# The first matrix product of six SwiGLU blocks computed as seven half-size products instead of eight

## The chip, the cores and the metric

The kernel runs on one core of a Trainium2 chip. The metric is the time of one execution on the device in microseconds (us); lower is better. Inputs and outputs lie in HBM. All arithmetic is in float32 or in pairs of float32r numbers.

## The reference, cut to what matters

The program is two stacks of layers over 512 tokens of width 1024. The first stack has two layers, each with a feed-forward block (FFN), a mixer and a second FFN, with a layer norm behind each; the second stack has two layers, each with a mixer and one FFN. So there are six FFNs, all of one shape, and they are what the change touches:

```python
D_MODEL = 1024; SEQ = 512; D_FF = 2816          # D_FF_2 of the second stack is 2816 too

def swiglu(x, w_in, w_out):
    gu = x @ w_in                               # 512x1024 by 1024x5632
    g, u = gu[..., :D_FF], gu[..., D_FF:]
    return (jax.nn.silu(g) * u) @ w_out         # 512x2816 by 2816x1024

# first stack, l = 0, 1
x = layer_norm(ALPHA * x + 0.5 * swiglu(x, ffn_w_in[l, 0], ffn_w_out[l, 0]), ln_g[l, 0], ln_b[l, 0])
x = layer_norm(ALPHA * x + mixer(x), ln_g[l, 1], ln_b[l, 1])
x = layer_norm(ALPHA * x + 0.5 * swiglu(x, ffn_w_in[l, 1], ffn_w_out[l, 1]), ln_g[l, 2], ln_b[l, 2])
# second stack, l = 0, 1
h = h + mixer_2(rms_norm(h, norm_mix[l]))
h = h + swiglu(rms_norm(h, norm_ffn[l]), w_ffn_in[l], w_ffn_out[l])
```

## The kernel before, in words

**Layout.** Activations lie transposed: eight tiles of 128 features by 512 tokens. `x` is the float32 value, `xh` and `xl` its two float32r parts (`split`: ScalarE copies to float32r, which gives the high part, VectorE subtracts it, which gives the low part). The tokens come in two halves, `HA` (0 to 255) and `HB` (256 to 511). A weight is split in the same way into `wh` and `wl`, and one product of two such numbers is three matmuls (`mm3`, lines 204 to 208): `wh` by `xh`, `wh` by `xl`, `wl` by `xh`. The weight is the stationary operand, the tokens move, and each matmul loads 128 by 128 weights of its own.

**An FFN** (`ffn`, line 272). The 2816 features of gate and of up are 22 tiles of 128 rows each. A weight unit is one tile of gate or up over all 1024 inputs: 128x1024 numbers, 512 KB, loaded by one DMA on SP's queue into one of three buffers `wr`, and split into one of three pairs `wh`, `wl`. A unit is 8 times `mm3`, 24 matmuls of 512 columns. When the up unit of a tile is done, `gate` makes silu(gate) on ScalarE (`sg`, line 281), the product with up on VectorE (`hf`, line 283) and its split `hh`, `hl`. `pre` (line 216) does the first four units in two passes, all of `HA` and then all of `HB`, in matmuls of 256 columns, because the norm of the layer ahead (`tail`, in the classes `LN` and `RMS`) ends with `HA` first and with `HB` while TensorE works on `HA`; the other 40 units are done by `gemms`, with the whole 512 tokens. Then `out_gemm` multiplies `hh`, `hl` by `w_out`.

**What sets the order.** The functions emit the work in one order with a clock of their own (`tick`, `run`); a scheduler of the framework then orders the instructions of each engine and sets the waits. VectorE, ScalarE and SP's queue work strictly in that order.

The FFNs are called from `program`: the first at the kernel's start, the second behind the first mixer, the third straight behind the second, the fourth behind the second mixer, the fifth and sixth in the second stack, with RMS norms, where `x` is the residual and the normed input lies in `xh` and `xl` alone.

Of the kernel before, what the change touches and what calls it, by code (L numbers as in the profile page):

```python
# [17 lines left out]
T = 512  # L18
D = 1024
KD = 8  # L20
NM = 22
# [3 lines left out]
HA, HB, HT = slice(0, 256), slice(256, 512), slice(0, 512)  # L25
# [6 lines left out]
FT = 2  # L32
PACE2, Y3 = 2.0, 1.0
MP, MF = 4, 3
AP, AF_, AK = 2, 3, 1
NP = 4
PACE = 2.0

SLOTS = [h for p in [(i, i + 4) for i in range(4)] + [(i + 8, i + 12) for i in range(4)] for h in p]
# [17 lines left out]
class Core:  # L57
# [128 lines left out]
    def weights(self, src, n=1024, at=None):  # L186

        w = self.raw(src, n)
        if at:
            for i in range(0, n, T):  # L190
                m = min(T, n - i)
                self.split(at[0][i // T][:, :m], at[1][i // T][:, :m], w[:, i:i + m])
            h, l = at
        else:
            h = self.wsp.tile([128, 1024], F32R, name="wh")
            l = self.wsp.tile([128, 1024], F32R, name="wl")
            self.split(h[:, :n], l[:, :n], w[:, :n])
        self.a(n)
        self.v(n)
        return h, l  # L200

    def mm3(self, out, w, k, xh, xl, start, stop):
        mm = self.nc.tensor.matmul
        wh, wl = (a[k // 4][:, k % 4 * 128:k % 4 * 128 + 128] if isinstance(a, tuple) else a[:, k * 128:(k + 1) * 128]
                  for a in w)
# [10 lines left out]
    def pre(self, srcs, ats=()):  # L216
# [12 lines left out]
        return ps  # L229
# [39 lines left out]
                            yield 0.65 * n / 512  # L269
                j[3](ps)  # L270

    def ffn(self, w_in, w_out, half, post, tail=None):

        nc, tc = self.nc, self.tc
        with tc.tile_pool(name="h", bufs=1) as hp:
            hh = [hp.tile([128, T], F32R, name=f"hh{m}") for m in range(NM)]
            hl = [hp.tile([128, T], F32R, name=f"hl{m}") for m in range(NM)]

            def gate(m, pg, pu):
                sg = hp.tile([128, T], F32, name="sg", bufs=2)  # L280
                nc.scalar.activation(sg, pg, AF.Silu)
                hf = hp.tile([128, T], F32, name="hf", bufs=2)
                nc.vector.scalar_tensor_tensor(hf, pu, half, sg, op0=OP.mult, op1=OP.mult)  # L283
                self.split(hh[m], hl[m], hf)
            first = [(m, j) for m in range(3) for j in range(2)][:NP]
            ats = [tuple(tuple(a[m:m + 2]) for a in (hh, hl)) for m in range(NM - 2, NM - 2 * (NP - 2), -2)]
            p0 = dict(zip(first, self.pre([w_in[m, :, j] for m, j in first], ats)))
            pend = {}

            def cb(m, j):  # L290
                def f(p):
                    pend[j] = p
                    if j:
                        gate(m, pend[0], p)
                return f
            for (m, j), p in p0.items():
                cb(m, j)(p)
# [4 lines left out]
    def out_gemm(self, w_out, hh, hl, nk, post, tail):  # L302

        self.run((self.out_head(w_out, hh, hl, nk, post, KD - tail), 1.0))
        self.out_tail(w_out, hh, hl, nk, post, tail)

    def out_part(self, o, u, w, hh, hl, s, first, last):
# [12 lines left out]
        if d == head - 1:  # L320
            self.later(post.mid(self, head), "mid")

    def out_head(self, w_out, hh, hl, nk, post, head):
        post.begin(self)
        seq = [(d, (i, min(i + 8, nk))) for d in range(head) for i in range(0, nk, 8)]
        held = {}
        for i, u in enumerate(seq):
            for v in seq[i:i + 2]:
                if v not in held:
                    held[v] = self.out_load(w_out, v)  # L330
            if i == len(seq) - 1:
                self.first_tail(w_out, nk, head)
            d, (k0, k1) = u
            if k0 == 0:
# [1185 lines left out]
def program(tc, d, out):  # L1520
    with ExitStack() as ctx:
        c = Core(ctx, tc, d["consts"])
        nc = tc.nc
        w0 = c.raw(d["w_in"][0][0, :, 0], 1024)
        c.ahead.append(w0)
        c.load_x(d["xT"], HA)

        def behind():
            c.load_x(d["xT"], HB)
            c.load_consts()  # L1530
        c.behind = behind
        b2 = Block2(ctx, c)
        with tc.tile_pool(name="b2t", bufs=1) as S:
            c.fill(S, 1216)
            c.later(b2.setup(S), "setup")
            c.ffn(d["w_in"][0], d["w_out"][0], 0.5, LN(c, 0))
            c.flush("setup")
        mlstm(c, d["ml_gate"], d["ml_qk"], d["ml_v"], d["ml_o"], d["ml_out"], LN(c, 1))
        c.ffn(d["w_in"][1], d["w_out"][1], 0.5, LN(c, 2))
        c.ffn(d["w_in"][2], d["w_out"][2], 0.5, LN(c, 3))  # L1540
        attn(c, d["at_q"], d["at_k"], d["at_v"], d["at_out"], LN(c, 4))
        c.ffn(d["w_in"][3], d["w_out"][3], 0.5, LN(c, 5, RMS(c.k("mix_g", 0, 8))), T4)
        for l in range(2):
            w = {n: d["b_" + n][l] for n in ("hf", "hq", "hg", "c", "hi", "nq", "kk", "vv", "w1", "out", "rope")}
            b2.layer(l, w, RMS(c.k("ffn_g", 8 * l, 8)))
            c.ffn(d["b_win"][l], d["b_wout"][l], 1.0, Out(out) if l else RMS(c.k("mix_g", 8, 8)))


def _ct(a, n=128):
# [125 lines left out]
```

## Time and profile before

| | us |
|---|---|
| median of 3 runs | 3350.05 (3348.68 to 3352.29) |
| profiled execution | 3350.13 |
| its span, first to last instruction | 3348.3 |
| TensorE matmul busy | 3305.9 (99% of the span), 18704 matmuls |
| TensorE weight load busy | 2827.0 (84%), beside the matmuls |
| VectorE busy | 1686.3 (50%) |
| ScalarE busy | 1280.9 (38%) |
| mean granted TensorE clock | 0.996 |

How to read it: a time in the timeline is from the start of the span; the duration of a matmul is longer than the distance to the next one's start, because matmuls are pipelined, so what a stream of them costs is read from the starts. `b` is a PSUM bank. A time in brackets is the engine's idle time ahead of an instruction, with what ended it.

### The profile page before, as it was taken

To read this page: it belongs to the slowest core of one execution; us is meant where nothing else is said; L and a number is where in the kernel's file an instruction comes from. 1 tells how busy PE (TensorE), PEld (TensorE's weight loads), DVE (VectorE), ACT (ScalarE), POOL (GpSimd) and SP (SyncE) were. 2 spreads that over 40 slices of the span, in tenths; PEclk is the share of its full clock that TensorE was granted. 3 is DMA by queue.
4 is the path that set the end of the run, shared out by engine and by line. 5 is a ranking of instruction groups with operands and counts; after the bars stand their busy time and mean duration, and the time that the engine had idled before them with its cause. 6 is when DMAs were issued, how large, how long until landed. Compare 5 with 4: busy or idle time off the path is not lost.

```text
span 3348.3 us, 46248 instructions
## 1 busy us (share of the span) xinstructions
PE 3305.9 (99%) x18704; PEld 2827.0 (84%) x18704; DVE 1686.3 (50%) x3451; ACT 1280.9 (38%) x2231; POOL 96.1 (3%) x138
## 2 busy tenths in 40 slices
PE   8999999999999999999999989999999999999999
PEld 7888977988898888879888978788888988898888
DVE  4333756733354333787334667775333567853332
ACT  3322545522233222685222433563232335632221
POOL 0000011000000000110000000000000000000000
PEclk9999999999999999999999989999999999999999
DMA  4333322233332333212333523112333332023333
GB/s 143 96 94 97 100 76 64 89 97 98 93 109 89 100 94 108 74 41 89 95 98 98 163 88 94 45 51 82 99 95 94 107 115 64 26 72 102 98 101 95
DMA packets 88918, 304.04 MB, mean 91 GB/s; under 512 B 9857, under 2 KB 12417, under 8 KB 88705
## 3 DMA queue, kind: packets, MB, share of 16 engines
q1 hardware_dynamic: 88704, 301.10, 29.3%
q8 instruction: 146, 2.39, 0.3%
q14 instruction: 68, 0.55, 0.0%
HBM read 298.96 MB, written 2.10 MB: 90 GB/s over the span
## 4 chain that ended last, share of the span: by engine, by line
PE 94%; DVE 3%; ACT 2%; DMA 1%; issue 1%; POOL 0%; DVEq 0%; SPq 0%; ACTq 0%; POOLq 0%
PE b L206 26%; PE b L208 26%; PE b L207 26%; PE b L267 2%; PE b L268 2%; PE b L266 2%; PE b L1250 1%; PE b L1442 1%; PE b L1391 1%; PE b L1420 1%; PE b L716 1%; ACT wh L174 1%; DVE wl L177 1%; PE b L1303 1%; DMA wr<-w_in 1%
## 5 line engine op out<-in xcount | busy, mean ns | idle before, releaser
L174 ACT ACTIVATE wh<-wr 128x1024 fp32r<-128x1024 f32 (+3 forms) x532 | 545.0, 1026 | 1568.1 <-PE b L207 980.5
L177 DVE TENSOR_TENSOR wl<-wr,wh 128x1024 fp32r<-128x1024 f32 (+3 forms) x532 | 628.3, 1183 | 867.2 <-ACT wh L174 864.9
L206 PE MATMUL b<-xh,wh 128*128 128x512 f32 (+1 forms) x2712 | 1021.7, 378 | 9.5 <-ACT xh L174 7.4
L208 PE MATMUL b<-xh,wl 128*128 128x512 f32 (+1 forms) x2712 | 1008.8, 373 | 3.2 <-DVE wl L177 3.2
L207 PE MATMUL b<-xl,wh 128*128 128x512 f32 (+1 forms) x2712 | 1008.7, 373 | 2.9 <-DVE xl L177 1.8
L206 PEld LDWEIGHTS b<-xh,wh 128*128 128x128 f32 x2712 | 511.1, 189 | 105.5 <-issue 9.4
L208 PEld LDWEIGHTS b<-xh,wl 128*128 128x128 f32 x2712 | 512.5, 189 | 94.5 <-DVE wl L177 5.8
L207 PEld LDWEIGHTS b<-xl,wh 128*128 128x128 f32 x2712 | 513.1, 189 | 91.7 <-issue 3.5
L206 PE MATMUL b<-hh,wh 128*128 128x512 f32 (+1 forms) x1144 | 400.4, 350 | 0.0
L208 PE MATMUL b<-hh,wl 128*128 128x512 f32 (+1 forms) x1144 | 398.4, 348 | 0.0
L207 PE MATMUL b<-hl,wh 128*128 128x512 f32 (+1 forms) x1144 | 398.3, 348 | 0.0
L283 DVE SCALAR_TENSOR_TENSOR hf<-b,sg 128x512 f32<-128x512 f32 x132 | 90.7, 691 | 407.4 <-PE b L208 404.0
L206 PEld LDWEIGHTS b<-hh,wh 128*128 128x128 f32 x1144 | 216.5, 189 | 28.6 <-issue 1.0
L207 PEld LDWEIGHTS b<-hl,wh 128*128 128x128 f32 x1144 | 216.5, 189 | 28.5 <-issue 1.0
L208 PEld LDWEIGHTS b<-hh,wl 128*128 128x128 f32 x1144 | 216.5, 189 | 27.6
L267 PE MATMUL b<-wl,xh 128*128 128x512 f32 (+2 forms) x352 | 122.8, 349 | 4.3 <-DVE wl L177 4.2
L266 PE MATMUL b<-wh,xh 128*128 128x512 f32 (+2 forms) x352 | 125.1, 360 | 0.0
L268 PE MATMUL b<-wh,xl 128*128 128x512 f32 (+2 forms) x352 | 122.7, 349 | 0.0
L177 DVE TENSOR_TENSOR hl<-hf,hh 128x512 fp32r<-128x512 f32 x132 | 89.9, 685 | 0.0
L174 ACT ACTIVATE hh<-hf 128x512 fp32r<-128x512 f32 x132 | 82.8, 632 | 0.8
L1395 ACT ACTIVATE sc<-sc,nm 128x128 f32<-128x128 f32 (+3 forms) x128 | 71.1, 557 | 23.5 <-DVE nm L1393 22.5
L267 PEld LDWEIGHTS b<-wl,xh 128*128 128x128 f32 x352 | 67.2, 191 | 14.3 <-DVE wl L177 6.1
(408 smaller groups left out, 4122.1 us busy)
## 6 DMA issues: line engine op xcount, KB each, us to landing
wr<-w_in SPq DMA_DIRECT2D x176, 512.0 KB, 3.7
wr<-b_win SPq DMA_DIRECT2D x88, 512.0 KB, 3.7
wr<-w_out SPq DMA_DIRECT2D x80, 512.0 KB, 3.5
wr<-b_wout SPq DMA_DIRECT2D x36, 512.0 KB, 3.5
wr<-w_out SPq DMA_DIRECT2D x36, 384.0 KB, 3.1
wr<-b_out SPq DMA_DIRECT2D x20, 512.0 KB, 3.6
wr<-b_w SPq DMA_DIRECT2D x16, 512.0 KB, 3.8
wr<-b_wout SPq DMA_DIRECT2D x16, 384.0 KB, 3.2
```

Of the source, the lines that this page charges most:

```text
L174: nc.scalar.activation(h, src, AF.Copy)
L177: nc.vector.tensor_sub(l, src, h.bitcast(F32))
L206: mm(out, wh, xh, start=start, stop=False)
L207: mm(out, wh, xl, start=False, stop=False)
L208: mm(out, wl, xh, start=False, stop=stop)
L266: mm(ps[t][:, :n], self.xh[k][:, ts], wh, start=k == 0, stop=False)
L267: mm(ps[t][:, :n], self.xh[k][:, ts], wl, start=False, stop=False)
L268: mm(ps[t][:, :n], self.xl[k][:, ts], wh, start=False, stop=k == KD - 1)
L283: nc.vector.scalar_tensor_tensor(hf, pu, half, sg, op0=OP.mult, op1=OP.mult)
L716: nc.tensor.matmul(p[:, :257], w[:, (j - j0) * 128:(j - j0 + 1) * 128], v[s][:, h], start=s == ss[0], stop=s == ss[-1])
L1250: nc.tensor.matmul(p[:, i * 64:(i + 1) * 64], K[h][:, ts], q, start=True, stop=True)
L1395: nc.scalar.activation(sc[:, :N], sc[:, :N], AF.Exp, bias=nm[:, g:g + 1], scale=-1.0, accum_out=sm[:, g:g + 1])
```

## The change

In every FFN 20 of the 22 tiles (ten pairs of tiles, `p` = 1 to 10) are computed by a scheme of seven products. Gate and up weights of a pair, each in two halves of the inputs, are the four blocks of a 2x2 matrix (`g(0)`: gate, inputs 0 to 511; `g(1)`: gate, the others; `g(2)`, `g(3)`: up); the input, in two halves of the inputs and two of the tokens, is the other (`b11` to `b22`). A product (`p1` to `p7`) is 256 rows by 512 inputs by 256 tokens: 2 times 4 times `mm3`, 24 matmuls of 256 columns, into one PSUM bank. Four sums of weights (`s2` and three in place, 128x1024 each) and eleven operations on the results (seven sums, two products and two copies or silus beside them) are made per pair, nearly all on VectorE. The results `h` stay float32 until the end of the loop and are then split by `halves`, ten times 128x1024. Four sums of the input (`t1` to `t4`, in `stage`) are made while `pre` works on `HB`; `t4` takes the place of `xh`, `xl` of the features 0 to 511 of `HB` once `pre` has read them. In the second stack the input is put together from `xh` and `xl` (`whole`) behind the end of each half. Weights come by DMAs of two times 512 numbers per row, through seven buffers. Tile pair 0 is still done by `pre`.

```diff
     def weights(self, src, n=1024, at=None):
         w = self.raw(src, n)
-        if at:
+        if at and not isinstance(at[0], tuple):
+            h, l = at
+            self.split(h[:, :n], l[:, :n], w[:, :n])
+        elif at:
...
         for s in (HA, HB):
             self.flush(s.start)
+            if then:
+                then(s)
             for k in range(KD):
...
-            self.run((self.gemms([("a", w_in[m, :, j], cb(m, j)) for m in range(NM) for j in range(2)
-                                  if (m, j) not in p0]), 1.0))
-            self.out_gemm(w_out, hh, hl, NM, post, tail or FT)
+            def whole(s):
+                for i, n in enumerate(parts):
+                    k0, t = parts[n]
+                    if normed and t is s:
+                        staged[n] = wide(f"h{1 + i}", dt=F32)
+                        for k in range(4):
+                            nc.vector.tensor_add(staged[n][:, k * 256:k * 256 + 256], self.xh[k0 + k][:, t].bitcast(F32),
+                                                 self.xl[k0 + k][:, t].bitcast(F32))
+            def stage():
...
+                for k in ks:
+                    sub(q("t1", k), g("b11", k), g("b12", k))
+                for k in ks:
+                    sub(q("t3", k), g("b22", k), g("b12", k))
+                for k in ks:
+                    stt(q("t2", k), q("t1", k), -1.0, g("b22", k), op0=OP.mult, op1=OP.subtract)
+                put("t2")
+                for k in ks:
+                    stt(q("t4", k), q("t2", k), -1.0, g("b21", k), op0=OP.mult, op1=OP.subtract)
+                put("t3")
+                put("t1")
+                staged["t4"] = o["t4"]
...
+            def weight(st):
+                p, x = st
+                g = lambda q: raws[p, q]
+                if x == "p6":
+                    held["s2", p] = wide("s2", dt=F32)
+                    nc.vector.tensor_add(held["s2", p], g(0), g(3))
+                elif x == "p5":
+                    nc.vector.tensor_add(g(2), g(2), g(3))
...
+                wh = self.wsp.tile([128, 1024], F32R, name="wh")
+                wl = self.wsp.tile([128, 1024], F32R, name="wl")
+                self.split(wh, wl, src)
+                if x == "p2":
+                    nc.vector.tensor_add(g(0), g(0), g(2))
+                elif x == "p7":
+                    nc.vector.tensor_add(g(1), g(1), held.pop(("s2", p)))
...
+            def product(st, w):
+                p, x = st
+                P[x] = self.bank()
+                for m in range(2):
+                    for k in range(4):
+                        wk = tuple(a[:, m * T + k * 128:m * T + k * 128 + 128] for a in w)
+                        self.mm3(P[x][:, m * 256:m * 256 + 256], wk, None, *moving(x, k), k == 0, k == 3)
+                        self.tick(0.36)
...
+            steps = [(p, x) for p in (1, 2) for x in ("p1", "p2")]
+            steps += [(p, x) for p in (1, 2) for x in ("p6", "p7", "p5", "p3", "p4")]
+            steps += [(p, x) for p in range(3, NP2) for x in ("p1", "p2", "p6", "p7", "p5", "p3", "p4")]
...
+            def then(s):
+                whole(s)
+                if s is HB:
+                    fetch()
+                    ahead(0, 2)
+                    stage()
...
+            for i, st in enumerate(steps):
+                ahead(i, 3)
+                product(st, ready.popleft())
+                after(st)
+                if i == len(steps) - 3:
+                    loaded[units[0]] = self.out_load(w_out, units[0])
+                    halves(5)
+                elif i == len(steps) - 2:
+                    loaded[units[1]] = self.out_load(w_out, units[1])
+                    halves(9)
+            self.out_gemm(w_out, hh, hl, NM, post, tail or FT, loaded, halves)
```

VectorE in the middle of the loop of the first FFN, before: one period, a gate tile and an up tile; `wl` is the low part of a weight unit.

```order
L177 TENSOR_TENSOR wl<-wr,wh 128x1024
L283 SCALAR_TENSOR_TENSOR hf<-b,sg 128x512
L177 TENSOR_TENSOR wl<-wr,wh 128x1024
L177 TENSOR_TENSOR hl_185<-hf,hh_163 128x512
L177 TENSOR_TENSOR wl<-wr,wh 128x1024
```

VectorE at the same place after: part of one pair. L377 (not shown) makes `s2`, L388, L379 and L386 are the sums of weights in place, L176 the low parts, the others work on results of products.

```order
L388 TENSOR_TENSOR wr<-wr,s_2169 128x1024
L176 TENSOR_TENSOR wl<-s_2169,wh 128x1024
L176 TENSOR_TENSOR wl<-wr,wh 128x1024
L417 TENSOR_TENSOR ga<-ua,b 128x512
L379 TENSOR_TENSOR wr<-wr,er 128x1024
L420 TENSOR_TENSOR ua<-ua,b 128x512
L176 TENSOR_TENSOR wl<-wr,wh 128x1024 x2
```

Two tiles took VectorE four low parts and four smaller operations; a pair now takes it seven low parts, four sums of weights and nine smaller operations.

VectorE at the start of the second FFN, before: the norm of `HB` ends with `xl_103` (feature tile 7), and the next are the low parts and gates of the loop.

```order
L465 TENSOR_TENSOR x_87<-x_87,b 128x256
L471 TENSOR_TENSOR xl_102<-x_86,xh_94 128x256
L471 TENSOR_TENSOR xl_103<-x_87,xh_95 128x256
L177 TENSOR_TENSOR wl<-wr,wh 128x1024
L283 SCALAR_TENSOR_TENSOR hf<-b,sg 128x512 x2
L177 TENSOR_TENSOR wl<-wr,wh 128x1024
```

The same place after, first where the norm of `HB` begins (L656 and L657 are its first two steps, 464 and 465 of before; `xl_96` is feature tile 0):

```order
L650 TENSOR_TENSOR lnr<-lnst,lnr 128x2
L176 TENSOR_TENSOR wl<-wr,wh 128x1024
L663 TENSOR_TENSOR xl_102<-x_86,xh_94 128x256
L386 TENSOR_TENSOR wr<-wr,er 128x1024
L663 TENSOR_TENSOR xl_103<-x_87,xh_95 128x256
L656 TENSOR_TENSOR x_80<-x_80,b 128x256
L176 TENSOR_TENSOR wl<-wr,wh 128x1024
L657 TENSOR_TENSOR x_80<-x_80,b 128x256
L656 TENSOR_TENSOR x_81<-x_81,b 128x256
L377 TENSOR_TENSOR s_6627<-wr,er 128x1024
L663 TENSOR_TENSOR xl_96<-x_80,xh_88 128x256
```

Four operations of 128x1024 now stand ahead of the first finished tile of `HB`. Then, where the norm has ended (`h_6418` is `t4`):

```order
L332 SCALAR_TENSOR_TENSOR h_6418<-h_6416,x_87 128x256
L176 TENSOR_TENSOR t3l<-h_6417,t3h 128x1024
L176 TENSOR_TENSOR t1l<-h_6415,t1h 128x1024
L176 TENSOR_TENSOR t2l<-h_6416,t2h 128x1024
L176 TENSOR_TENSOR xl_96<-h_6418,xh_88 128x256
L176 TENSOR_TENSOR xl_97<-h_6418,xh_89 128x256
L176 TENSOR_TENSOR xl_98<-h_6418,xh_90 128x256
L176 TENSOR_TENSOR xl_99<-h_6418,xh_91 128x256
L464 SCALAR_TENSOR_TENSOR ga<-b,ga 128x512 x2
L176 TENSOR_TENSOR wl<-wr,wh 128x1024
```

The last row is the low part of the weights of the third product (`p1` of pair 2); the low parts of the first two products stand in the piece above it, and the whole of `stage` and the gates of tiles 0 and 1 stand ahead of the third.

## Rows read from the trace of the kernel before

**Rows 1.** The page: busy time of engines, and the last chain by engine.

```profile
PE 3305.9 (99%) x18704; PEld 2827.0 (84%) x18704; DVE 1686.3 (50%) x3451; ACT 1280.9 (38%) x2231; POOL 96.1 (3%) x138
...
PE 94%; DVE 3%; ACT 2%; DMA 1%; issue 1%; POOL 0%; DVEq 0%; SPq 0%; ACTq 0%; POOLq 0%
```

**Rows 2.** Waits of TensorE: total us, times, longest; the three largest.

```profile
PE b L206 <- ACT xh L174: 7.4, 2, 6.4
PE b L398 <- DVE lns L489: 6.2, 1, 6.2
PE b L267 <- DVE wl L177: 4.2, 2, 2.1
```

**Rows 3.** Timeline, TensorE, loop of the first FFN: start, duration, instruction; 16 matmuls.

```profile
59.50 0.39 PE L208 MATMUL b<-xh,wl 128*128 128x512 f32 x1
...
63.12 0.39 PE L206 MATMUL b<-xh,wh 128*128 128x512 f32 x1
```

**Rows 4.** Timeline, TensorE, `pre` of the second FFN: its last 15 matmuls.

```profile
648.12 0.28 PE L206 MATMUL b<-xh,hh 128*128 128x256 f32 x1
...
649.80 0.28 PE L208 MATMUL b<-xh,hl 128*128 128x256 f32 x1
```

**Rows 5.** Timeline, VectorE, loop of the first FFN: a low part and the next instruction.

```profile
58.12 1.22 DVE L177 TENSOR_TENSOR wl<-wr,wh 128x1024 fp32r<-128x1024 f32 x1 [0.15 <-ACT wh L174]
59.26 0.68 DVE L177 TENSOR_TENSOR hl<-hf,hh 128x512 fp32r<-128x512 f32 x1
```

**Rows 6.** Timeline: VectorE's smaller operations, each row a run back to back; ScalarE's copy.

```profile
349.78 2.47 DVE L438 TENSOR_TENSOR x<-x,b 128x512 f32<-128x512 f32 x4
...
624.32 0.75 DVE L442 TENSOR_TENSOR x<-x,b 128x256 f32<-128x256 f32 x2
...
62.47 1.06 ACT L174 ACTIVATE wh<-wr 128x1024 fp32r<-128x1024 f32 x1 [3.83 <-PE b L207]
```

**Rows 7.** Timeline, VectorE, start of the second FFN: the norm of `HB`, first and last.

```profile
634.15 0.16 DVE L458 TENSOR_TENSOR lnr<-lnst,lnr 128x2 f32<-128x2 f32 x1 [0.81 <-POOL lnr L457]
...
645.45 0.42 DVE L471 TENSOR_TENSOR xl<-x,xh 128x256 fp32r<-128x256 f32 x1 [0.70 <-ACT x L469]
```

**Rows 8.** The same at the start of the third FFN: end of the norm, then the loop.

```profile
1013.66 0.43 DVE L471 TENSOR_TENSOR xl<-x,xh 128x256 fp32r<-128x256 f32 x1 [0.70 <-ACT x L469]
1018.22 1.23 DVE L177 TENSOR_TENSOR wl<-wr,wh 128x1024 fp32r<-128x1024 f32 x1 [4.13 <-ACT wh L174]
```

**Rows 9.** Timeline, VectorE and TensorE, start of the fifth FFN (RMS norm).

```profile
2290.80 0.99 DVE L177 TENSOR_TENSOR xl<-sq,xh 128x256 fp32r<-128x256 f32 x2
...
2301.76 0.28 PE L208 MATMUL b<-xh,hl 128*128 128x256 f32 x1
```

**Rows 10.** Timeline, VectorE, start of the first FFN.

```profile
34.27 1.23 DVE L177 TENSOR_TENSOR wl<-wr,wh 128x1024 fp32r<-128x1024 f32 x1 [12.29 <-ACT wh L174]
```

**Rows 11.** Stretches: length; busy us of PE, PEld, DVE, ACT, POOL; clock, DMA share, GB/s.

```profile
1965.00:1966.00 1.00, 0.00 (x0) 0.00 (x0) 0.97 (x3) 0.99 (x3) 0.00 (x0) 1.00 0.00 0
...
1968.00:1969.00 1.00, 1.00 (x4) 0.79 (x3) 1.00 (x2) 0.16 (x1) 0.00 (x0) 0.59 0.78 270
1969.00:1970.00 1.00, 1.00 (x3) 0.72 (x3) 1.00 (x3) 0.00 (x0) 0.00 (x0) 0.50 0.89 250
1970.00:1971.00 1.00, 1.00 (x4) 0.80 (x3) 0.31 (x1) 0.00 (x0) 0.00 (x0) 0.50 0.66 176
1971.00:1972.00 1.00, 1.00 (x5) 0.81 (x4) 0.00 (x0) 0.00 (x0) 0.00 (x0) 0.70 0.98 385
```

**Rows 12.** Timeline, VectorE, `out_gemm` of the second FFN.

```profile
890.06 1.23 DVE L177 TENSOR_TENSOR wl<-wr,wh 128x1024 fp32r<-128x1024 f32 x1 [4.69 <-ACT wh L174]
```

**Rows 13.** Stretches again: the loop of the first FFN; two us at the kernel's start.

```profile
40.00:280.00 240.00, 240.00 (x1060) 198.75 (x1059) 81.28 (x88) 68.04 (x85) 0.00 (x0) 1.00 0.33 99
...
18.00:20.00 2.00, 2.00 (x19) 2.00 (x19) 1.97 (x7) 0.00 (x0) 0.00 (x0) 1.00 0.90 266
```

More of the change, by code (lines that the diff above doesn't have):

```diff
@@ L35 @@
 AP, AF_, AK = 2, 3, 1
-NP = 4
 PACE = 2.0
@@ L270, in gemms, with ffn @@
                 j[3](ps)
-    def ffn(self, w_in, w_out, half, post, tail=None):
+    def ffn(self, w_in, w_out, half, post, tail=None, normed=False):
         nc, tc = self.nc, self.tc
+        NP2 = NM // 2
         with tc.tile_pool(name="h", bufs=1) as hp:
[L276 to L297, printed above, removed]
-            self.run((self.gemms([("a", w_in[m, :, j], cb(m, j)) for m in range(NM) for j in range(2)
-                                  if (m, j) not in p0]), 1.0))
-            self.out_gemm(w_out, hh, hl, NM, post, tail or FT)
@@ new lines, in moving @@
+            def moving(n, k):
+                if n in ("p1", "p2"):
+                    k, s = (k, HA) if n == "p1" else (k + 4, HA)
+                elif n in ("p3", "p4"):
+                    k, s = (k + 4, HB) if n == "p3" else (k, HB)
+                else:
+                    a, b = form[{"p5": "t1", "p6": "t2", "p7": "t3"}[n]]
+                    return a[:, k * 256:k * 256 + 256], b[:, k * 256:k * 256 + 256]
+                return self.xh[k][:, s], self.xl[k][:, s]
+            loads = deque((p, q) for ps in [(1, 2)] + [(p,) for p in range(3, NP2)] for qs in ((0, 1), (2, 3))
+                          for p in ps for q in qs)
@@ new lines, in ffn, with fetch @@
+            slots, raws, n = [None] * 7, {}, [0]
+            def fetch():
+                while loads:
+                    i = n[0] % 7
+                    if slots[i] is not None:
+                        return
+                    p, q = slots[i] = loads.popleft()
+                    w = self.wraw.tile([128, 1024], F32, name="wr") if i < 3 else wide("er", 4, F32)
+                    j, r = divmod(q, 2)
+                    nc.sync.dma_start(w.rearrange("p (m c) -> p m c", m=2),
+                                      w_in[2 * p:2 * p + 2, :, j, r * T:r * T + T].rearrange("m p c -> p m c"))
+                    raws[p, q] = w
+                    n[0] += 1
@@ new lines, in ffn, with ahead @@
+            steps = [(p, x) for p in (1, 2) for x in ("p1", "p2")]
+            steps += [(p, x) for p in (1, 2) for x in ("p6", "p7", "p5", "p3", "p4")]
+            steps += [(p, x) for p in range(3, NP2) for x in ("p1", "p2", "p6", "p7", "p5", "p3", "p4")]
+            ready = deque()
+            def ahead(i, k):
+                while len(ready) < k and i + len(ready) < len(steps):
+                    ready.append(weight(steps[i + len(ready)]))
+            def then(s):
+                whole(s)
+                if s is HB:
+                    fetch()
+                    ahead(0, 2)
+                    stage()
@@ new lines, in ffn @@
+            ats = [(wide(f"h{i}"), wide(f"h{i - 1}")) for i in (10, 8, 6)]
+            ps = self.pre([w_in[m, :, j] for m in range(2) for j in range(2)], ats, then)
+            for k in range(4):
+                self.split(self.xh[k][:, HB], self.xl[k][:, HB], staged["t4"][:, k * 256:k * 256 + 256])
+            hh, hl = [], []
+            pair = wide("hh0"), wide("hl0")
+            for m in range(2):
+                sg = hp.tile([128, T], F32, name="ga", bufs=2)
+                nc.scalar.activation(sg, ps[2 * m], AF.Silu)
+                nc.vector.scalar_tensor_tensor(sg, ps[2 * m + 1], half, sg, op0=OP.mult, op1=OP.mult)
+                for a, o in zip(pair, (hh, hl)):
+                    o.append(a[:, m * T:m * T + T])
+                self.split(hh[m], hl[m], sg)
@@ new lines, in ffn, with halves @@
+            names = [None, "t2h", "t2l", "t3h", "t3l", "t1h", "t1l", "s2"] + ["er"] * 4
+            def halves(k):
+                while len(hh) <= k:
+                    p = len(hh) // 2
+                    a = [wide(n, 4 if n == "er" else 1) for n in (names[p], names[11] if p == 1 else f"h{p - 1}")]
+                    self.split(*a, h[p])
+                    for i, o in zip(a, (hh, hl)):
+                        o.extend(i[:, m * T:m * T + T] for m in range(2))
+            units = [(0, (i, min(i + 8, NM))) for i in (0, 8)]
@@ L305, in out_gemm @@
+    def out_gemm(self, w_out, hh, hl, nk, post, tail, loaded=None, need=None):
+        self.run((self.out_head(w_out, hh, hl, nk, post, KD - tail, loaded, need), 1.0))
         self.out_tail(w_out, hh, hl, nk, post, tail)
@@ L321, in out_done, with out_head @@
             self.later(post.mid(self, head), "mid")
-    def out_head(self, w_out, hh, hl, nk, post, head):
+    def out_head(self, w_out, hh, hl, nk, post, head, loaded=None, need=None):
         post.begin(self)
         seq = [(d, (i, min(i + 8, nk))) for d in range(head) for i in range(0, nk, 8)]
-        held = {}
+        held = loaded or {}
         for i, u in enumerate(seq):
@@ L333, in out_head @@
             d, (k0, k1) = u
+            if need:
+                need(k1 - 1)
             if k0 == 0:
```

73 lines of the change are left out of this document (68 added, 5 removed).

## The prediction, made before the changed kernel had run

> **What bounds the kernel now.** I read the page's busy times first and its chain of waits second. TensorE is busy for 3305.9 us of a span of 3348.3, and it holds 94% of the chain that ended last [rows 1]. The list of waits says what is left: the three longest entries are 7.4, 6.2 and 4.2 us, and all of them together are about 40 us [rows 2]. So the time is TensorE's stream of matmuls, and the change has to be read in two places: how far that stream gets shorter, and where VectorE, at 50% today, can no longer keep ahead of it.
>
> **The loop, TensorE's side.** A matmul of 512 columns costs the distance to the next start: 16 of them lie between 59.50 and 63.12, so 0.2267 us each [rows 3]. Of 256 columns there are 14 distances between 648.12 and 649.80, so 0.120 us each, in `pre`, with a new 128x128 weight for every one, as in a product [rows 4]. The stretch of the loop shows a clock of 1.00 [rows 13]. A pair of tiles takes 4 units of 24 matmuls now, 96 × 0.2267 = 21.76 us. Afterwards it takes 7 products of 24 short ones, 168 × 0.120 = 20.16 us. That is 1.60 us less for a pair and, for ten pairs in six FFNs, **−96 us**. The columns alone (7 for 8) would give 21.76 / 8 = 2.72 a pair; the short matmul costs more than half of the long one, and over 1 us of that goes there.
>
> [...]
>
> **The loop, VectorE's side.** What a low part costs in a row of work is 59.26 − 58.12 = 1.14 us, with a shown duration of 1.22 [rows 5]. Four operations of 512 in a run take 2.47, with 0.68 for one, so (2.47 − 0.68) / 3 = 0.60; two of 256 take 0.75, with 0.42 for one [rows 6, 7], so 0.33 to 0.42, and I take 0.36. Now a pair needs 4 × 1.14 + 4 × 0.60 = 7.0 of 21.76 us. Afterwards it needs seven low parts, four sums of weights and nine smaller operations: 11 × 1.14 + 9 × 0.60 = 17.9 of 20.16 us, 89%. ScalarE's seven copies and three smaller ones stay under 10 × 1.06 = 10.6 [rows 6]. So TensorE still covers both and the loop pays nothing for the sums. Order matters inside a pair, since the low parts are used in sequence: adding up the operations as VectorE's order has them, the tightest places are `p6`, whose weights are done 5.15 us behind the pair's start and needed at 2 × 2.88 = 5.76, and `p5`, done at 10.7 and needed at 11.52. If every instruction took its full duration, VectorE would need 11 × 1.225 + 9 × 0.69 = 19.7, and one wait of about 0.7 for ScalarE's copy behind a sum makes 20.4; then the cover is gone and the loop pays 0.24 × 60 = 14 us. The copy of `p1`'s result waits on ScalarE with the next weights' copies queued behind it, but those are three products ahead. So 0, with 14 as the upper bound.
>
> **The starts of the FFNs.** Here the new work is not covered, because VectorE's order puts it ahead of what TensorE needs soon. In the second FFN VectorE starts its last norm steps at 634.15 and ends the norm of `HB` at 645.45 + 0.42 = 645.87 [rows 7]. Between the first of these and the low part of the third product's weights there now stand in addition 8 operations of 1024 (two low parts, two sums of weights, three low parts of `stage`, the low part itself), 20 of 256 (`t1` to `t4`, the split of `t4`) and two first gates: 8 × 1.14 + 20 × 0.36 + 2 × 0.60 = 17.5 us. Idle pieces such as the 0.81 and 0.70 in these rows take up about 1.5 of it, so it ends at 645.87 + 17.5 − 1.5 = 661.9. TensorE ends `pre` at 649.80 + 0.12 = 649.92 [rows 4], has two products ready (5.76 us) and uses the low part 0.24 later: 655.9. It waits 6.0 us. That some of the first product's matmuls are drawn into `pre` changes nothing in this sum. If no idle piece is filled it waits 7.5, if twice as much is, 4.5.
>
> The third FFN has three more operations of 1024 there and stalls one product later: 1014.09 + 11 × 1.14 + 7.2 + 1.2 − 1.5 = 1033.5 [rows 8] against 1018.13 + 3 × 2.88 + 0.24 = 1027.0, so 6.5, and 1.2 more at `p6`, whose low part is one operation behind: 7.7. The fourth is built like the second: 6.0. In the fifth the norm ends at 2290.80 + 0.99 = 2291.79; behind that stand 12 operations of 1024, 20 of 256 (16 of `whole`, 4 of the split of `t4`) and three of 512, 22.7 us, to 2314.5, against 2301.76 + 0.12 + 5.76 + 0.24 = 2307.9 [rows 9]: 6.6. The sixth is the same. The first FFN has no norm ahead of it and VectorE idles 12.29 us just there [rows 10]: 0, at most 3. With 0.6 for the low part of pair 1's `p5` in five FFNs: 6.0 + 7.7 + 6.0 + 6.6 + 6.6 + 3.0 = **+36 us**, between 27 and 45.
>
> A wait can cost more than its length. TensorE waited 2.1 us [rows 2] around 1965, the clock still 1.00; three us later the granted clock is 0.59, 0.50, 0.50 and 0.70 in four stretches of 1 us, with TensorE busy throughout [rows 11]. So it ran at the lower level (1.2 GHz) for part of them and lost 0.41 + 0.50 + 0.50 + 0.30 = 1.7 us. If each of the five waits is followed by the same, that is **+8.5 us**; 0 if none is (that row is one case), 17 if it is twice as long.
>
> **The ends.** Ten splits of `h` are new on VectorE, 11.4 us, and stand behind the last `p5`, with 6 × 0.60 = 3.6 of the last results and about 5.5 of low parts of `w_out`: 20.5 us until the last `h` is split. TensorE meanwhile has `p3` and `p4` (5.76) and two and a half units of `w_out` at 24 × 0.2267 = 5.44, together 19.4. That leaves about 1 us for an FFN, **+6 us**; 0 if the order lets the splits in earlier, 3 each (18) if the copies on ScalarE are late too. After that VectorE idles 4.69 us ahead of a unit [rows 12], so nothing lasts.
>
> **The sum**, against the profiled execution, 3350.13, which is 0.08 above the median: 3350.1 − 96 + 36 + 8.5 + 6 = 3304.6, so **3305 us**. Its own bounds are 3350.1 − 96 + 27 = 3281 and 3350.1 − 96 + 45 + 17 + 18 = 3334, and 3348 with the loop's 14.
>
> **Rivals.**
> - *The starts are hidden.* If VectorE's order leaves the new work no place on TensorE's path (more idle pieces ahead of the norm of `HB` than I count), the 36 and 8.5 fall: 3260. For it speaks that TensorE has 5.76 us of products in hand; against it, that 17 to 23 us of new work meet about 10 us of cover. Chance 0.12.
> - *VectorE holds the loop, slower than before.* If every instruction waits for the end of the one ahead, a pair takes VectorE 19.7 us, and the waits of `s2` and `g(2)`'s sum for ScalarE's copies add about 2.1: 21.8. From 20.16 on each us of this is lost on TensorE, and from 21.76 on, where the loop's gain is gone, it decides for slower. At these prices each of five starts takes 2 us longer too: 3350.1 + 2 + 36 + 10 + 8.5 + 6 = 3413. Against it stands that the row at 59.26 starts before 58.12 + 1.22 has passed [rows 5]. Chance 0.06. The Trainium skill (VectorE: DVE Perf Modes, section "The DRAIN you can't avoid") says that the next operation does not start until the pipe is empty, and adds that one that is not held starts earlier. The first alone would make this rival; the row, with 0.08 us of overlap, agrees with the second.
> - *Weights come late at the start.* SP has seven loads of 512 KB to bring there, 3.67 MB, at some 266 GB/s [rows 13] 13.8 us, and the sums at lines 386 and 377 wait for the fifth and the sixth while the norm of `HB` is queued behind them on VectorE and `pre`'s second pass behind that. If the loads cannot start early, each of five starts costs some 7 us more: 3340. For it: they stand ahead of the norm in VectorE's order. Against: SP has nothing else before that, and in the loop the DMAs are busy for 0.33 of the time [rows 13]. Chance 0.10.
> - *The change does not do what it says:* the short matmul costs 0.130 us in the loop, 168 × 0.130 = 21.84, because its weight load no longer hides; then 3350.1 + 5 + 50 = 3405. Rows 4 show it hidden. Chance 0.02.
> - *The short matmul costs half of the long one* (0.1133 us), and `pre` is held up by something else: 163 us saved, 3350.1 − 163 + 50.5 = 3238. Against it: 14 equal distances with no wait [rows 4]. Chance 0.03. [...]
>
> **How the numbers follow.** The forecast has 0.67, and I give its bounds 3281 to 3334 some 0.6 of that. To leave out no more than 2 in 10 the range must take in hidden starts (3260) and late weights (3340): 3258 to 3342, which holds about 0.82. About 0.2% (6.7 us) is what a measurement can tell from no change. Faster by more: the forecast but for its upper end (0.65), hidden starts 0.12, half of the late weights 0.05, cheap matmuls 0.03: 0.85. Slower: VectorE's rival, the one on weight loads, and 0.01 of the rest: 0.09. Within 0.2%: 0.06.
>
> **What would show it.** In the changed profile: product matmuls 0.120 us apart and a pair every 20.16 us, at a clock of 1.00; VectorE busy for about 89% of the loop; TensorE waits of 6 to 8 us for a low part (line 176) some 6 to 9 us into the loops of FFN two to six, none in the first; a clock of 0.50 for some us after each; small waits at the ends. The prediction is wrong if TensorE has many short waits for line 176 in the loop, if the distance is not 0.120, or if the starts show no wait or one of over 10 us.

## The result, and the profile after

| | before | after |
|---|---|---|
| median, us | 3351.13 (3348.68 to 3352.29) | 3289.61 (3288.51 to 3290.45) |
| span of the profiled run | 3348.3 | 3286.8 |
| mean granted clock | 0.996 | 0.993 |

The changed kernel is faster: ratio 0.9817, interval 0.98 to 0.9834, 61.5 us less in the spans too. The forecast was 3305 with a range of 3258 to 3342: the sign and the range hold, and the gain was 16 us larger than forecast.

The page of the changed kernel, busy time and last chain by engine; the rows of before are [rows 1]:

```profile
PE 3222.3 (98%) x23024; PEld 2965.5 (90%) x23024; DVE 2465.1 (75%) x4371; ACT 1520.3 (46%) x2449; POOL 98.1 (3%) x138
...
PE 88%; DVE 6%; ACT 2%; issue 2%; DMA 1%; POOL 1%; POOLq 0%; SPq 0%; DVEq 0%; ACTq 0%
```

TensorE has more matmuls in less time, VectorE went from 50% to 75%, and its share of the chain from 3% to 6%: TensorE still sets the time, but no longer everywhere.

**The loop** went as forecast. The timeline of TensorE in the first FFN: the first matmul of `p6` in three pairs, and three in a row.

```profile
80.18 0.28 PE L208 MATMUL b<-t2h,wh 128*128 128x256 f32 x1
...
100.34 0.28 PE L208 MATMUL b<-t2h,wh 128*128 128x256 f32 x1
100.46 0.28 PE L209 MATMUL b<-t2l,wh 128*128 128x256 f32 x1
100.58 0.28 PE L210 MATMUL b<-t2h,wl 128*128 128x256 f32 x1
...
120.50 0.28 PE L208 MATMUL b<-t2h,wh 128*128 128x256 f32 x1
```

A pair takes 20.16 us, matmuls stand 0.12 apart. Busy time by stretch, columns as in [rows 13], six pairs:

```profile
100.00:220.96 120.96, 120.96 (x1011) 120.96 (x1010) 109.44 (x121) 54.03 (x61) 0.00 (x0) 1.00 0.30 97
```

TensorE has no gap and VectorE is busy for 109.44 / 120.96 = 90% of it (89% forecast). So the loops gave 60 × 1.60 = 96 us, and the other 96 − 61.5 = 34.5 were given back elsewhere (50.5 forecast).

**Where it was given back.** The first matmul of `out_gemm` in the first two FFNs, before:

```profile
252.84 0.39 PE L206 MATMUL b<-hh,wh 128*128 128x512 f32 x1
...
868.60 0.39 PE L206 MATMUL b<-hh,wh 128*128 128x512 f32 x1
```

And after:

```profile
235.70 0.40 PE L208 MATMUL b<-hh,wh 128*128 128x512 f32 x1
...
843.20 0.40 PE L208 MATMUL b<-hh,wh 128*128 128x512 f32 x1
```

The first FFN thus gained 17.1 us (16 of the loop and 1.1 of small waits that are gone), and from there to the same place in the second there are 607.50 us instead of 615.76: 8.3 less where the loop gives 16, so 7.7 were lost on the way. For FFN 2 to 6 the same sum gives 7.7, 8.2, 5.1, 7.3 and 7.3, in all 35.6; behind the last of these matmuls, 125.24 us remain against 125.21. What TensorE loses in the five starts beyond what it lost there before adds up as follows: about 17 us in waits behind `pre`, 8 us in waits in `pre` or just ahead of it, and 12 us by which matmuls behind the waits stand further apart than 0.120. That is 37, within 2 us of the 35.6. The 17 are 20.7 less 3.5: the kernel before lost 0.7 us at the head of each loop, and that is gone.

The start of the second FFN shows all three. VectorE's timeline, from the last norm step that [rows 7] begins with, to the low part of the third product's weights:

```profile
616.65 0.16 DVE L650 TENSOR_TENSOR lnr<-lnst,lnr 128x2 f32<-128x2 f32 x1 [0.81 <-POOL lnr L649]
618.95 1.23 DVE L176 TENSOR_TENSOR wl<-wr,wh 128x1024 fp32r<-128x1024 f32 x1 [2.14 <-ACT wh L173]
...
633.99 0.43 DVE L663 TENSOR_TENSOR xl<-x,xh 128x256 fp32r<-128x256 f32 x1
...
638.36 1.22 DVE L176 TENSOR_TENSOR t3l<-h,t3h 128x1024 fp32r<-128x1024 f32 x1
...
643.11 1.28 DVE L464 SCALAR_TENSOR_TENSOR ga<-b,ga 128x512 f32<-128x512 f32 x2
644.31 1.22 DVE L176 TENSOR_TENSOR wl<-wr,wh 128x1024 fp32r<-128x1024 f32 x1
```

ScalarE there: the copies of the first and of the third product's weights, and the table load of the gates.

```profile
617.86 1.06 ACT L173 ACTIVATE wh<-wr 128x1024 fp32r<-128x1024 f32 x1 [2.45 <-DMA wr<-w_in]
...
636.87 1.28 ACT L463 ACT_TABLE_LOAD   x1
...
641.31 1.05 ACT L173 ACTIVATE wh<-wr 128x1024 fp32r<-128x1024 f32 x1
```

TensorE there: the end of the first two products, and the first matmuls of the third to the fifth.

```profile
640.77 0.28 PE L210 MATMUL b<-xh,wl 128*128 128x256 f32 x1
642.42 0.39 PE L208 MATMUL b<-xh,wh 128*128 128x256 f32 x1 [1.37 <-ACT wh L173]
...
643.85 0.38 PE L208 MATMUL b<-xh,wh 128*128 128x256 f32 x1 [0.93 <-ACT wh L173]
...
644.79 0.58 PE L208 MATMUL b<-t2h,wh 128*128 128x256 f32 x1 [0.45 <-ACT wh L173]
...
645.58 0.58 PE L210 MATMUL b<-xh,wl 128*128 128x256 f32 x1
```

And the clock behind it, in stretches of 2 us:

```profile
644.00:646.00 2.00, 1.55 (x6) 1.07 (x7) 2.00 (x3) 1.78 (x3) 0.00 (x0) 0.56 0.00 0
646.00:648.00 2.00, 2.00 (x11) 2.00 (x11) 2.00 (x4) 0.00 (x0) 0.00 (x0) 0.50 0.00 0
648.00:650.00 2.00, 2.00 (x11) 2.00 (x10) 2.00 (x3) 0.00 (x0) 0.00 (x0) 0.50 0.00 0
650.00:652.00 2.00, 2.00 (x14) 2.00 (x14) 1.18 (x2) 1.54 (x3) 0.00 (x0) 0.73 0.03 8
```

The low part of the third product's weights starts at 644.31, and the matmul that reads it at 645.58. From 640.89 on TensorE could do six matmuls (0.72 us), so it lost about 4.0 us there. Then it is busy at a clock of 0.50, and 11 matmuls stand in 2 us instead of 17.

In the list of TensorE's waits (total us, times, longest) ScalarE's copies of weights end more of this time than VectorE's low parts; all 17 waits of the two entries lie in the five starts:

```profile
PE b L208 <- ACT wh L173: 13.5, 13, 2.2
PE b L210 <- DVE wl L176: 4.2, 4, 1.7
```

That does not make ScalarE the limit. TensorE's order lets the first two matmuls of each of the next products pass while the third product's low part is missing, and each of these pairs then waits for its own copy; the low part still comes last. No single wait is of the 6 to 8 us that the prediction gave as its sign; they are at most 2.2 us.

### The profile page after: what moved, and what is told of

It is laid out like the page before. It is cut to its first block, busy times and chain, and to the rows that moved or that the text cites. A ratio compares the mean times of both kernels' runs of the same rounds, so it can differ in the third digit from the quotient of the medians.

```text
span 3286.8 us, 56333 instructions
## 1 busy us (share of the span) xinstructions
PE 3222.3 (98%) x23024; PEld 2965.5 (90%) x23024; DVE 2465.1 (75%) x4371; ACT 1520.3 (46%) x2449; POOL 98.1 (3%) x138
## 4 chain that ended last, share of the span: by engine, by line
PE 88%; DVE 6%; ACT 2%; issue 2%; DMA 1%; POOL 1%; POOLq 0%; SPq 0%; DVEq 0%; ACTq 0%
PE b L208 24%; PE b L210 24%; PE b L209 24%; PE b L272 2%; PE b L273 2%; PE b L271 2%; PE b L1442 1%; PE b L1634 1%; PE b L1583 1%; PE b L1612 1%; DVE wl L176 1%; PE b L908 1%; DMA wr<-w_in 1%; ACT wh L173 1%; PE b L1495 1%
## 5 line engine op out<-in xcount | busy, mean ns | idle before, releaser
L173 ACT ACTIVATE wh<-wr 128x1024 fp32r<-128x1024 f32 (+2 forms) x454 | 459.9, 1017 | 761.5 <-PE b L209 541.1
L176 DVE TENSOR_TENSOR wl<-wr,wh 128x1024 fp32r<-128x1024 f32 (+2 forms) x454 | 530.9, 1173 | 348.9 <-ACT wh L173 347.6
L208 PE MATMUL b<-xh,wh 128*128 128x256 f32 (+1 forms) x2520 | 769.7, 307 | 15.2 <-ACT xh L173 7.7
L210 PE MATMUL b<-xh,wl 128*128 128x256 f32 (+1 forms) x2520 | 756.5, 301 | 4.3 <-DVE wl L176 4.2
L209 PE MATMUL b<-xl,wh 128*128 128x256 f32 (+1 forms) x2520 | 755.4, 300 | 4.3 <-DVE xl L663 2.4
L209 PE MATMUL b<-h,wh 128*128 128x512 f32 (+1 forms) x936 | 326.0, 348 | 0.0
L173 ACT ACTIVATE wh<-er 128x1024 fp32r<-128x1024 f32 x186 | 194.3, 1056 | 174.4 <-PE b L209 97.0
L176 DVE TENSOR_TENSOR wl<-er,wh 128x1024 fp32r<-128x1024 f32 x186 | 225.0, 1219 | 8.2 <-ACT wh L173 8.2
L209 PEld LDWEIGHTS b<-h,wh 128*128 128x128 f32 x936 | 177.2, 189 | 24.2 <-DVE h L176 1.0
L208 PE MATMUL b<-t1h,wh 128*128 128x256 f32 (+1 forms) x584 | 173.7, 298 | 0.9 <-ACT wh L173 0.9
```

Source lines behind the costliest of these rows:

```text
L173: nc.scalar.activation(h, src, AF.Copy)
L176: nc.vector.tensor_sub(l, src, h.bitcast(F32))
```

## Experiments

Theory: the price is the queue of VectorE and ScalarE at the starts, with the lower clock that follows each wait. Rivals: late weights; a loop that VectorE holds; a clock that falls for another reason.

**The stage left out** (`no_stage`).

```diff
                 else:
-                    a, b = form[{"p5": "t1", "p6": "t2", "p7": "t3"}[n]]
-                    return a[:, k * 256:k * 256 + 256], b[:, k * 256:k * 256 + 256]
+                    s = HB
...
                     ahead(0, 2)
-                    stage()
...
-            for k in range(4):
-                self.split(self.xh[k][:, HB], self.xl[k][:, HB], staged["t4"][:, k * 256:k * 256 + 256])
```

> The four sums of the input (t1 to t4) and their splits are left out; p5, p6 and p7 move xh and xl of HB instead, and t4 does not take their place. So VectorE has about 10.6 us less and ScalarE about 4.5 us less to do at the start of each FFN, all else stays. Theory (the queue of VectorE and ScalarE at the starts is the price): of the 35.6 us that FFN 2 to 6 take above the loop's gain, the waits of TensorE behind pre (17) and the low clock behind them (12) go: 3261, between 3256 and 3268. Rival (late weights, or the sums of weights ahead of the norm, set the starts): less than half of it goes, 3275 or more.

Measured: 3258.9 (3256.28 to 3259.09), ratio 0.9723 (0.9708 to 0.9737). The matmuls behind `pre` stand 0.12 apart in all six FFNs from the first product on, no wait for a weight of the loop is left in the list, and the mean clock is 0.997. So about 30 us hang on the stage's work; the waits in `pre` or just ahead of it stayed, about 2 us for each of FFN 2 to 6.

**The weights of the first products loaded earlier** (`er_first`).

```diff
-                    w = self.wraw.tile([128, 1024], F32, name="wr") if i < 3 else wide("er", 4, F32)
+                    w = wide("er", 4, F32) if i < 4 else self.wraw.tile([128, 1024], F32, name="wr")
```

> The first four weight loads of the scheme in each FFN go to the four buffers that are free early (er), the next three to wr; before it is three to wr, which wait for pre's weights, then four to er. In the second FFN of the changed kernel (3289.6 us) the loads of er were issued at 607.46 us, those of wr from 610.77, and ScalarE stood 2.45 us until 617.86 for the first product's weights with the norm of HB queued behind it. Theory (late weights are a part of the price of the starts): that wait goes, the norm of HB ends about 2 us earlier in FFN 2 to 6 and the waits in pre (about 8 us in all) get smaller: 3280, 7 to 12 us less. Rival (VectorE's queue alone sets the starts, the idle piece only moves): 3289, within 3 us.

Measured: 3291.6 (3289.53 to 3293.34), ratio 0.982 (0.9804 to 0.9836): no gain. ScalarE's copy did come earlier, in the second FFN of this run:

```profile
613.64 1.06 ACT L173 ACTIVATE wh<-er 128x1024 fp32r<-128x1024 f32 x1 [0.83 <-DMA er<-w_in]
```

But the order that the scheduler made of it puts more of the loop's weights ahead of the norm of `HB`: seven operations of 1024 start on VectorE between 616.75 and 629.42, where the changed kernel has four ahead of the norm's end, and the norm's last low part stands at 638.25, where it had stood at 633.99. So the late load was real (2.45 us), but the idle time that it left was filled with work that the norm then had to wait for. As the order changed together with the load, the run does not show what the late load costs by itself.

**The wait filled** (`fill`).

```diff
+            filler = self.seen > 0
+            self.seen += 1
...
                 ahead(i, 3)
+                if i == 2 and filler:
+                    idle = self.bank()
+                    for k in range(8):
+                        for j in range(3):
+                            nc.tensor.matmul(idle[:, HA], wlast[:, k * 128:k * 128 + 128], self.xh[k][:, HA], start=True, stop=True)
+                wlast = ready[0][0]
                 product(st, ready.popleft())
```

> In FFN 2 to 6, 24 matmuls of 256 columns whose result nobody reads stand between the second and the third product, 2.88 us at 0.120, where TensorE waits 3.2 to 4.8 us and then runs at a clock of 0.50 for some us. Theory (the lower clock follows from the wait): with the wait filled the clock stays at 1.00 and about 2.4 us a start come back, less what of the 24 sticks out: 3280, between 3277 and 3285. Rival (the clock falls for another reason, or the waits that remain are enough): the lower clock stays and the time is 3289 to 3295.

Measured: 3288.4 (3287.51 to 3290.92), ratio 0.9814 (0.9799 to 0.9828), so no gain in time, but behind `pre` the clock did what the theory says in four of the five starts. The second FFN, columns as above:

```profile
644.00:646.00 2.00, 1.35 (x12) 1.15 (x10) 2.00 (x4) 1.83 (x3) 0.00 (x0) 1.00 0.00 0
646.00:648.00 2.00, 1.97 (x14) 1.78 (x15) 1.94 (x4) 1.02 (x2) 0.00 (x0) 1.00 0.03 8
```

Over the five starts the excess distances behind `pre` fall from 12 us to about 3 and the waits from 17 to about 6, some 20 us; the 120 extra matmuls cost 5 × 2.88 = 14.4. About 4 us come back in `pre` of the fourth and the sixth FFN, where waits of 1.2 and 2.1 us are followed by a clock of 0.50, and 1.5 in the first FFN, which has no extra matmuls. In the fifth FFN, where waits of 0.67 and 0.82 us within 2 us are left, the clock falls to 0.50 once more. So the lower clock follows the waits, though not every wait: two of 1.04 and 1.07 us within 2 us, in the third FFN of `late_gate` (below), left it at 1.00. A wait filled with idle work of its own length only trades one for the other.

**The first gates behind the third product** (`late_gate`).

```diff
-            for m in range(2):
+            def first():
+                for m in range(2):
...
                 product(st, ready.popleft())
+                if i == 2:
+                    first()
```

> The gates of tiles 0 and 1 (two silus with a table load of 1.28 us on ScalarE, two products and splits on VectorE) are emitted behind the third product and no longer ahead of it. Theory (ScalarE's copy of the third product's weights, at 641.31 us in the second FFN, stands behind them and TensorE waits for it and for VectorE's low part): that product starts 1.2 to 2.5 us earlier in FFN 2 to 6, and the stretch at the lower clock gets shorter: 3280, between 3276 and 3284. Rival (the four banks of pre are held longer, and the fifth product waits for one instead): 3288 to 3295.

Measured: 3277.9 (3276.45 to 3281.15), ratio 0.9782 (0.9768 to 0.9797). 11.7 us for moving two gates that nobody needs there: the wait is the third product's weights, standing behind them on two engines. The list of waits shows which of the two comes last. The entries that were 4.2 and 13.5 us are now:

```profile
PE b L210 <- DVE wl L176: 8.1, 5, 2.4
...
PE b L208 <- ACT wh L173: 2.3, 5, 0.6
```

With the gates and their table load out of its way ScalarE is nearly in time, and what is left is mostly VectorE's low part. The rival's wait shows once: in the third FFN 1.04 us ahead of the sixth product end with the ScalarE copy that empties the bank of `p1`.

**The splits of the stage moved behind products too** (`late_all`).

```diff
-                put("t2")
...
-                put("t3")
-                put("t1")
                 staged["t4"] = o["t4"]
+                late.extend([lambda: put("t2"), lambda: put("t3"), lambda: put("t1")])
...
+                if i == 2:
+                    first()
+                elif i in (0, 1, 3):
+                    late.pop(0)()
+                elif i == 4:
+                    for k in range(4):
+                        self.split(self.xh[k][:, HB], self.xl[k][:, HB], staged["t4"][:, k * 256:k * 256 + 256])
```

> As late_gate (3277.9 us), and the splits of the input's sums are spread over the first products: t2 behind the first, t3 behind the second, the gates behind the third, t1 behind the fourth, t4 behind the fifth. So VectorE makes the low part of the third product's weights straight behind the sums t1 to t4. Theory (the wait at the starts is the third product's weights standing behind the stage in VectorE's and ScalarE's order, not the stage itself): in late_gate TensorE still waits 1.5 to 3.4 us behind pre in FFN 2 to 6 and loses 0.6 to 2.7 us to the lower clock; most of these 22 us go: 3260, between 3256 and 3268. Rival (VectorE has no room in the first pairs: 35.8 us of loop work and 7.4 us of splits in 40.3 us): the waits come back at the fifth to seventh product: 3274 to 3285.

Measured: 3273.3 (3272.03 to 3279.27), ratio 0.9775 (0.9758 to 0.9791). The rival was the better forecast, and the 4.6 us against `late_gate` are hardly clear of noise, since the two intervals overlap. The wait at the third product of the second FFN is gone, and a new one stands at the seventh, whose weights now come behind the moved splits and gates:

```profile
652.83 0.39 PE L208 MATMUL b<-t1h,wh 128*128 128x256 f32 x1 [0.82 <-ACT wh L173]
653.77 0.39 PE L208 MATMUL b<-xh,wh 128*128 128x256 f32 x1 [0.44 <-ACT wh L173]
```

**Spread further** (`late_more`: `t1` behind the third product, `t4` behind the sixth, the gates behind the tenth) **and eight sums on GpSimd** (`late_pool`: in addition, in the fifth and sixth FFN; the last two lines). The edit is shown against `late_all`.

```diff
-                if i == 2:
+                if i == 9:
                     first()
-                elif i in (0, 1, 3):
+                elif i in (0, 1, 2):
                     late.pop(0)()
-                elif i == 4:
+                elif i == 5:
...
-                            nc.vector.tensor_add(staged[n][:, k * 256:k * 256 + 256], self.xh[k0 + k][:, t].bitcast(F32),
+                            (nc.gpsimd if s is HA else nc.vector).tensor_add(staged[n][:, k * 256:k * 256 + 256], self.xh[k0 + k][:, t].bitcast(F32),
```

> As late_all (3273.3 us), with t1 behind the third product, t4 behind the sixth and the gates only behind the tenth, so that these 3.8 us of VectorE and 2.9 us of ScalarE no longer stand ahead of the weights of the seventh product. Theory (what is left at the starts is VectorE's backlog in the first pair): in late_all TensorE waits 1.6 to 2.5 us there in FFN 2 to 6 and loses 0.8 to 2.5 to the lower clock; of these 19 us 10 to 16 go: 3261, between 3257 and 3265. Rival (the work only moves, pairs 2 and 3 have no room for it): 3270 to 3276.

> As late_more, and in FFN 5 and 6 the eight sums that put the input of HA together (128x256 each) run on GpSimd, which is idle there, not on VectorE: 8 x 0.36 = 2.9 us less on VectorE ahead of the loop. Theory (VectorE's queue is what TensorE waits for at these two starts): 2 to 4 us less than late_more. Rival (these sums lie in idle time of VectorE, or GpSimd is too slow for the half): the same time as late_more or up to 10 us more.

Measured: 3269.4 (3268.3 to 3270.86), ratio 0.9764 (0.9747 to 0.978), and 3264.9 (3263.44 to 3266.04), ratio 0.9749 (0.9734 to 0.9763). The kernel before took 3348.3 us beside these runs and 3350.5 beside those of `late_all`, so some 2 of the 3.9 us between `late_all` and `late_more` lie in the runs, and the rest is not clear of noise: the rival (the work only moves) was the nearer forecast. In the first two pairs of the five starts about 6 us of waits are left of 11, but 0.9 us each came back in the third pair. With `late_pool` the waits in the first two pairs of the fifth and sixth FFN are gone, and these two FFNs give 4.2 of the 4.6 us that it gains over `late_more`. It is the fastest kernel here, 25 us faster than the changed kernel, or 22 with each measured against the kernel before beside it.

**More sums on VectorE** (`sum_1`, `sum_3`; with one sum the tuple holds `p4` alone).

```diff
+                if x in ('p1', 'p3', 'p4'):
+                    nc.vector.tensor_add(wide("s2", dt=F32), g({"p1": 0, "p3": 1, "p4": 3}[x]), g({"p1": 0, "p3": 1, "p4": 3}[x]))
                 src = {"p1": lambda: g(0), "p2": lambda: g(1), "p6": lambda: held["s2", p], "p7": lambda: g(0),
```

> One sum more of 128x1024 on VectorE for each pair of tiles, whose result nobody reads. Theory (VectorE is covered in the loop, 17.9 of 20.16 us for a pair): 19.1 of 20.16, the period of a pair stays 20.16 and the time is 3289 to 3296. Rival (VectorE already holds the loop): each pair takes 1.14 longer, 68 us in all, 3358.

> Three sums more of 128x1024 on VectorE for each pair of tiles, whose results nobody reads. Theory (cover of 2.2 us for a pair): 17.9 + 3.4 = 21.3 us of VectorE are more than TensorE's 20.16, the period becomes 21.3 to 21.5 and the time 3360 to 3380, with the lower clock on top where waits are long. Rival (VectorE can pack more than the shown distances say): 3300 or less.

Measured: 3290.9 (3290.29 to 3291.47), ratio 0.9822 (0.9802 to 0.9841), and 3390.3 (3388.6 to 3392.04), ratio 1.0118 (1.0098 to 1.0139). The stretch of six pairs with one sum more, and with three:

```profile
100.00:220.96 120.96, 120.96 (x1010) 120.96 (x1009) 115.70 (x127) 53.52 (x60) 0.00 (x0) 1.00 0.30 97
```

```profile
100.00:228.94 128.94, 125.14 (x1011) 121.87 (x1010) 128.25 (x140) 54.38 (x60) 0.00 (x0) 1.00 0.29 91
```

With one more VectorE is at 96% and TensorE has no gap. With three it is at 99% and a pair takes 21.49 us (`p6` starts at 104.91, 126.39 and 147.89), 21.3 forecast: 60 × 1.33 = 80 us. The 20 us more, where the forecast gave little, are spread: about 6 in the loops, 6 in `pre` and 9 between the end of a loop and the next `pre`. So the loop of the changed kernel had room for one such operation per pair and not for three; two were not tried.

**The kernel before with short matmuls** (`cols256`).

```diff
-                for k in range(KD):
-                    self.mm3(p, w, k, self.xh[k], self.xl[k], k == 0, k == KD - 1)
-                    yield 0.65
+                for s in (HA, HB) if len(j) > 3 else (slice(0, T),):
+                    for k in range(KD):
+                        self.mm3(p[:, s], w, k, self.xh[k][:, s], self.xl[k][:, s], k == 0, k == KD - 1)
+                        yield 0.65 * (s.stop - s.start) / T
...
-            self.run((self.gemms([("a", w_in[m, :, j], cb(m, j)) for m in range(NM) for j in range(2)
+            self.run((self.gemms([("a", w_in[m, :, j], cb(m, j), 2) for m in range(NM) for j in range(2)
```

> The kernel before, with eight products, but the 40 units of each FFN's loop in two passes of 256 columns instead of one of 512. Theory (a short matmul costs 0.120 us, over half of 0.2267): a unit takes 48 x 0.120 = 5.76 us instead of 5.44, 240 units 77 us more: 3427. Rival (the short matmul costs half of the long one, and other things made it look longer): 3350.

Measured: 3425.8, ratio 1.0224 (1.0204 to 1.0245), 75 us slower. The same multiplications and the same bytes: this is what halving the columns costs, and seven eighths of it is what the scheme pays out of its eighth of the multiplications.

## Why the forecast was right, and where its terms were off

- **What bounds the kernel, and the loop (−96):** right: 20.16 us a pair, 0.120 a matmul, as worked out from [rows 3, 4]. `cols256` shows the price of the short matmul by itself. The Trainium skill (TensorE: Matmul & The Clock Gate, "Back-to-back issue gap") has a table of 262 cycles for 256 columns and 518 for 512, which it gives for a single matmul by itself and not for a stream with weight loads. Carried over to this stream it would make an estimated 143 us; the streams here show 288 and 544 cycles of the full clock, and none shows its 262.
- **VectorE covered in the loop:** right; 90% busy against 89%, and `sum_1` and `sum_3` put the edge between 19.1 and 21.3 us of VectorE's work for a pair of 20.16. The rival in which VectorE holds the loop falls with `sum_1`, which cost nothing.
- **The waits at the starts (+36):** the mechanism was right (`no_stage`, `late_gate`), the size too large: about 17 us behind `pre` and 8 in it or just ahead, 25 in all. The 0.7 us that each loop's head had lost before were not taken off, which is 3.5 of the 11. The step that failed is the term of 6 to 7.7 us for each start, in which TensorE's cover was held fixed. From the norm step at 616.65 VectorE took 28.9 us to the end of that low part, where the sum has 661.9 − 634.15 = 27.8: its side was right within 1.1 us, in part by luck, since 2.1 us of it are idle time ahead of 618.95 that the sum did not have. But TensorE was busy until 640.89, 24.2 us behind that step, where I had counted 649.92 + 5.76 − 634.15 = 21.5. Of the 2.7 more, 0.9 is a wait of its own inside `pre` (at 620.57), since the weights' work placed in the norm delays the last tiles of `HA` as well. Most of the rest is 1.5 us of `pre` that TensorE's order has ahead of the norm's next step, which stands at 618.11. Part of the forecast wait so became a wait in `pre`, and part was covered. This was worked out for the second FFN alone.
- **The clock (+8.5):** the mechanism was right, the size too small: about 12 us, 1.6 to 2.9 for a start where [rows 11] gave 1.7. `fill` shows the link: with the wait filled the clock behind `pre` stays at 1.00 in four of five starts.
- **The ends (+6):** wrong, 0. The 396 matmuls of 512 columns with which `out_gemm` of the second FFN begins take 89.6 us from the first start to the last, 89.5 before, with no wait in them or ahead of them: the order let the splits of `h` in early enough (the first starts at 835.36, 7.8 us ahead of `out_gemm`), the lower bound of that term.
- **The first FFN (0 to 3):** −1.1 in the profiled execution; I had left out that its small waits of before could go. In `fill`, whose first FFN is the same work, it is +0.4, so this is no more than runs differ by.
- **Rivals:** "weights come late" is half true: a load did hold ScalarE for 2.45 us with the norm behind it, but taking most of that away (`er_first`) changed the time by nothing that can be told, with VectorE's order changed along with it. "Hidden starts" did not happen, though `late_pool` (3264.9) comes near its 3260 by reordering.

Together: waits 11 less, clock 3 more, ends 6 less and the first FFN 1 less make 15, and the distance of the spans' 61.5 from the 45.5 forecast is 16. The misses mostly add up; only the clock's went the other way. What stays open is what the 8 us of waits in `pre` are due to one by one; they were in `no_stage` as well.

## What to carry to other kernels

Price a scheme that multiplies less by the instruction that it ends up with: seven eighths of the columns were 12.5% less, and with the shorter matmul the loop became only 7.4% shorter. Then look at the places where the engine that took over the sums has no lead yet: the loop was free, and over a third of its gain was lost in the five starts. There it pays to ask of every instruction in the queue who needs it first: moving gates and splits behind products that do not read them, and eight sums to an idle engine, brought 22 to 25 us with no work taken away.

## What the runs showed of the hardware

- In each of the five starts of the changed kernel two or three waits of 0.4 to 2.2 us in a row were followed by 3 to 7 us at a granted clock of 0.50 (the lower level, 1.2 GHz), most of it with TensorE busy. That cost 1.6 to 2.9 us a start, 12 in all beside 17 of waits.
- A matmul of 256 columns takes 0.120 us, 53% of one of 512 (0.2267), whether each is part of a product or half of one that was split (`cols256`).
- With VectorE busy for 96% of a loop TensorE had no gap (`sum_1`); with more work than fits, VectorE was busy for 99% and set the loop's pace (`sum_3`).
